# Gate and up products by Strassen's scheme (7 for 8), with the output projection of all tokens ahead of the FFN

## Chip, core and metric

The kernel runs on one NeuronCore of a Trainium2 chip. Its time is device microseconds, the median of several executions. A second view is one execution recorded by the hardware profiler; "the profile" and "the trace" below mean that one. PE is TensorE (PEld its weight loads), DVE VectorE, ACT ScalarE, POOL GpSimd, SP the engine whose queue issues the DMAs.

## What is computed

One inference step of a one-layer decoder: a mixer (four retention heads and four gated-delta heads on one normalised stream), an output projection, a layer norm, a SwiGLU feed-forward network (FFN), another layer norm. There are 2048 prompt tokens, 16 meta tokens (whose FFN output isn't asked for) and 32 sample tokens (8 x 4); D_MODEL is 1024, D_FF 2816. What matters here is the end:

```python
mixed = concatenate([o_r, o_g], -1) @ w_out            # 1024 x 1024
h = layer_norm(ALPHA * h + mixed, ln1_g, ln1_b)
gu = h @ w_gate_up                                     # 1024 x 5632
f = (silu(gu[..., :D_FF]) * gu[..., D_FF:]) @ w_down   # 2816 x 1024
y = layer_norm(ALPHA * h + f, ln2_g, ln2_b)
```

All inputs are float32. A matmul here takes each operand as a high part (a cast to float32r) and a low part (what is left), and adds three products, high x high, high x low, low x high. That is `mm3`; the split into two parts is `split`, a cast on ACT and a subtraction on DVE or POOL.

## The kernel before

`attention` goes first: four blocks of 512 prompt tokens, whose mixer outputs go to memory (`mixd`) with the normalised stream (`xhat`). Its code is the same before and after.

`ffn` then runs `ffn_block` for two blocks of tokens: 1056 (the 32 sample tokens and 1024 prompt tokens, nine tiles) and 1024 (eight tiles). A block has these stages:

- Output projection, a tile of 128 tokens at a time: `load(i)` brings the tile's mixer output and splits it, `project(i)` does 48 matmuls of 512 columns, adds the residual (L1105) and takes the layer norm, `transposed(i)` turns the tile on PE (L1113) and writes its split parts into `fxT`, which stays in SBUF for the block.
- Gate and up, for f from 0 to 21 (128 columns of gate and 128 of up each; the text calls one f a slice): `gateup(f)` loads 1 MB of weights as two raw halves, splits them (ACT, DVE), and for each group of 352 columns (first block) or 512 (second; 256 in the last two slices) does 2 x 24 matmuls into two PSUM tiles `g0` and `g1`; tanh on ACT (L1127) and two products on DVE (L1128, L1129) make the SwiGLU value, split on ACT and POOL into `ff`.
- Down, for each pair of slices: `down(g)` takes each tile and half of the model width, six matmuls of 512 columns, and adds to `y` on DVE (L1147). It runs behind the first slice of the next pair, so a whole slice of gate/up lies between its operands and its use.
- `finish(i)`: layer norm and store. In the second block the last two slices go in quarters with down and finish between them.

A layer norm (`layer_norm`) is two statistics (L212), a dozen one-column operations (L189 to L196, L225), an ACT pass (L228), a DVE product (L230) and two POOL additions (L232).

The order of instructions on each engine is not the order of the code: a scheduler lays them out at compile time, by the program's order as priority and by when it reckons that operands and buffers are ready. On the chip each engine takes its list strictly in that order. A tag with `bufs=n` has n buffers; a new tile of the tag waits until an old one has been read by all its readers. All DMAs are issued on SP.

Of the kernel before, what the change touches and what calls it, by code (L numbers as in the profile page):

```python
# [35 lines left out]
LAG = 3  # L36
# [112 lines left out]
class _Cut:  # L149


    def __init__(self, pool, full, n):
        self.pool, self.full, self.n = pool, full, n
# [10 lines left out]

class Builder:
# [124 lines left out]
    def mm3(self, out, lh, ll, rh, rl, kn, first=True, last=True):  # L290

        for k in range(kn):
            for i, (a, b) in enumerate(((lh, rh), (lh, rl), (ll, rh))):
                self.nc.tensor.matmul(out, lhsT=a(k), rhs=b(k), start=first and k == 0 and i == 0, stop=last and k == kn - 1 and i == 2)  # L294


    def setup(self):
        nc, I = self.nc, self.I
        cp = self.pool("const")
        self.wring = self.pool("wring", bufs=2)  # L300
        self.wcols = 8 * 264
        self.raw = self.pool("raw", bufs=2)
        self.dr = self.pool("dram", space=DRAM)
# [760 lines left out]
    def ffn_block(self, tiles, groups, bi):  # L1064

        nc = self.nc
        T = sum(r for _, r, _ in tiles)
        NT = len(tiles)
        TM = NS + 1024
        with ExitStack() as s:  # L1070
            xp, fp, tp = self.fxp, self.ffp, self.ftp
            pg, pd, pt = self.pg, self.pd, self.pt
            sm = self.fsm
            ff = lambda dt=F32: fp.tile([128, TM], dt, tag="ff", name="ff")
            y = [(self.fyp if i < 6 else xp).tile([128, D], F32, tag=f"y{i}", name=f"y{i}") for i in range(NT)]
            xT = xp.tile([128, 2, 8, TM], F32R, tag="fxT", name="fxT")
            xh, xl = xT[:, 0, :, :T], xT[:, 1, :, :T]
            vec = lambda i: self.vec_bcast(i, fp, "ff")
            mixed, wo = {}, {}

            def load(i):
                r0, rows, c0 = tiles[i]
                blk, off = self.mix_pos(r0)
                raw = ff()[:, :1024].rearrange("p (k n) -> p k n", k=8)[:, :, :rows]
                nc.sync.dma_start(out=raw, in_=self.mixd[blk][:, :, off:off + rows].rearrange("k p n -> p k n"))
                nc.sync.dma_start(out=y[i][:rows], in_=self.xhat_rows(r0, rows))
                if bi and i < NT // 2:

                    o = tiles[NT - 1 - i][2]
                    hh, ll = xh[:, :, o:o + rows], xl[:, :, o:o + rows]  # L1090
                else:
                    hh, ll = [ff(F32R)[:, :1024].rearrange("p (k n) -> p k n", k=8)[:, :, :rows] for _ in range(2)]
                self.split(raw, hh, ll, "act", "dve")
                mixed[i] = hh, ll

            def project(i):
                r0, rows, c0 = tiles[i]
# [8 lines left out]
                self.layer_norm(y[i][:rows], rows, g1, b1, sm)  # L1106

            def transposed(i):
                r0, rows, c0 = tiles[i]
                for j in range(2):  # L1110
# [3 lines left out]
                    self.split(p[:, :, :rows], xh[:, 4 * j:4 * j + 4, c0:c0 + rows], xl[:, 4 * j:4 * j + 4, c0:c0 + rows], "act", "dve")  # L1114

            def gateup(f, w=None, o=None, gs=None):
                wh, wl = w or self.piece(self.I["gu"][f])
                fh, fl = o or (ff(F32R)[:, :T], ff(F32R)[:, :T])
                for c, n in gs or groups:
                    ps = []  # L1120
                    for u in range(2):
                        p = pg.tile([128, 512], F32, tag=f"g{u}", name=f"g{u}")[:, :n]
                        ps.append(p)
                        q = 128 * u
                        self.mm3(p, lambda k: wh[:, k, q:q + 128], lambda k: wl[:, k, q:q + 128], lambda k: xh[:, k, c:c + n], lambda k: xl[:, k, c:c + n], 8)
                    t = tp.tile([128, 512], F32, tag="th", name="th")[:, :n]
                    nc.scalar.activation(out=t, in_=ps[0], func=AF.Tanh, scale=0.5)  # L1127
                    nc.vector.scalar_tensor_tensor(out=t, in0=t, scalar=1.0, in1=ps[0], op0=ALU.add, op1=ALU.mult)  # L1128
                    nc.vector.scalar_tensor_tensor(out=t, in0=t, scalar=0.5, in1=ps[1], op0=ALU.mult, op1=ALU.mult)  # L1129
                    self.split(t, fh[:, c:c + n], fl[:, c:c + n], "act", "pool")  # L1130
                return fh, fl

            def down(g, fs, w=None, sel=None, lag=0):
                wh, wl = w or self.piece(self.I["dn"][g])
                wv = [w.rearrange("p a b -> p (a b)") for w in (wh, wl)]
                for i in sel or range(NT):
                    r0, rows, c0 = tiles[i]
                    for n in range(2):
                        p = pd.tile([128, 512], F32, tag="d", name="d")[:rows]
                        o = 512 * n  # L1140
                        self.mm3(p, lambda f: fs[f][0][:, c0:c0 + rows], lambda f: fs[f][1][:, c0:c0 + rows],
# [6 lines left out]
                    if lag and i >= lag:  # L1148
                        finish(i - lag)

            def finish(i):
                r0, rows, c0 = tiles[i]
                self.layer_norm(y[i][:rows], rows, g2, b2, sm, bi and i == NT - 1)
                nc.sync.dma_start(out=self.O["y"][r0:r0 + rows, :], in_=y[i][:rows])

            for n in range(2):
                for kk in range(2):
                    wh, wl = self.piece(self.I["wout"][n, kk])
                    r = lambda w: w.rearrange("p a b -> p (a b)").rearrange("p (a b) -> p a b", a=4)
                    wo[n, kk] = r(wh), r(wl)  # L1160
                    if n + kk == 0:
                        load(0)
            load(1)
            g1, b1 = vec(2), vec(3)
            for i in range(NT):
                project(i)
                if i and i + 1 < NT:
                    load(i + 1)
                if i > bi:
                    transposed(i - bi - 1)  # L1170
                if self.late:
                    self.late.pop(0)()

            ng = NF // 2
            w = self.piece(self.I["gu"][0])
            f0 = ff(F32R)[:, :T], ff(F32R)[:, :T]
            gateup(0, w, f0, groups[:-1])
            for i in range(NT - bi - 1, NT):
                transposed(i)
            gateup(0, w, f0, groups[-1:])  # L1180
            fs = [f0, gateup(1)]
            for g in range(ng - 1):
                if g == ng - 2:
                    g2, b2 = vec(4), vec(5)
                    if bi:
                        break
                nxt = [gateup(2 * g + 2)]
                down(g, fs)
                nxt.append(gateup(2 * g + 3))
                fs = nxt  # L1190
            if bi:

                w = [self.piece(self.I["gu"][NF - 2 + u]) for u in range(2)]
                down(ng - 2, fs)
                fs = [(ff(F32R)[:, :T], ff(F32R)[:, :T]) for u in range(2)]
                wd = self.piece(self.I["dn"][ng - 1])
                q = T // 4
                for i in range(4):
                    for u in range(2):
                        gateup(NF - 2 + u, w[u], fs[u], [(q * i, q)])  # L1200
                        if i:
                            down(ng - 1, fs, wd, [2 * i - 2 + u])
                            if 2 * i - 2 + u:
                                finish(2 * i - 3 + u)
                for i in (6, 7):
                    down(ng - 1, fs, wd, [i])
                    finish(i - 1)
                finish(NT - 1)
            else:
                down(ng - 1, fs, lag=LAG)  # L1210
                self.late = [lambda i=i: finish(i) for i in range(NT - LAG, NT)]

# [13 lines left out]
    def piece(self, src):  # L1226
        self.np = getattr(self, "np", 0) + 1
        return self.load_piece(src, ring=self.wring if self.np % 2 else self.wring2)

    def ffn(self):  # L1230
        with ExitStack() as s:
            self.wring2 = self.pool("wring2", bufs=2, es=s)
            self.ffp = self.pool("f_f", bufs=7, es=s)
# [34 lines left out]
```

## Time and profile before

| what | value |
|---|---|
| time, median of 3 runs | 3127.39 us (3121.61 to 3128.01) |
| the profiled execution's own time | 3126.54 us |
| its span, first to last instruction | 3124.8 us |
| mean granted TensorE clock | 0.982 |
| PE, PEld busy | 2992.5 us (96%), 2589.8 us (83%) |
| DVE, ACT, POOL busy | 1708.0 (55%), 882.4 (28%), 548.6 us (18%) |
| first output-projection matmul | at 1348.2 us |
| moved by DMA | 309.41 MB, 99 GB/s in the mean |

A busy PE in this table is not PE at its peak, since matmuls overlap in the record; the distance from one matmul's start to the next one's is the better measure. A digit of the page's slices is the busy tenth of one fortieth of the span, 78 us. An idle time "<- DVE y L1147" was ended by that instruction.

### The profile page before, as it was taken

The page shows a single profiled execution, that of the slowest core. Times are in us where ns is not written, and L with a number is a line of the kernel's source. Part 1 is how long each engine was busy: PE and PEld are TensorE (multiplying, and loading weights), DVE is VectorE, ACT ScalarE, POOL GpSimd, SP SyncE. Part 2 cuts the span into 40 slices and gives each one's busy share as a digit, 9 for nine tenths or more (in the row PEclk, how much of TensorE's full clock was granted, in tenths as well). Part 3 has the DMA queues.
Part 4 walks back from the last instruction along what each step waited for, and adds up shares of the span by engine and source line. Part 5 has one row for each costly group of instructions (what it writes and reads, how often), then busy time and mean ns, then how long its engine had stood idle before and what let it go on. Part 6 is the DMA issues. An engine that isn't in the chain of part 4 may idle for free. (4 is left out here: it accounts for less than half of the span.)

```text
span 3124.8 us, 44640 instructions
## 1 busy us (share of the span) xinstructions
PE 2992.5 (96%) x17858; PEld 2589.8 (83%) x17858; DVE 1708.0 (55%) x3922; ACT 882.4 (28%) x2083; POOL 548.6 (18%) x570
## 2 busy tenths in 40 slices
PE   7999998999999989999999999999999999999997
PEld 6888887888888877878999999988777877878787
DVE  7777676766666676667333333333684333333346
ACT  2444433444443434333111111111233111111111
POOL 1332222221222131112101111110241000001002
PEclk8999998999999999999999999999999999999999
DMA  7534543443434333252111111112242111111111
GB/s 255 222 139 173 179 151 127 149 147 144 154 144 149 117 116 117 92 167 75 41 54 41 41 52 44 41 46 63 84 134 81 41 54 41 54 41 54 41 41 55
DMA packets 96592, 309.41 MB, mean 99 GB/s; under 512 B 11472, under 2 KB 39680, under 8 KB 80000
## 3 DMA queue, kind: packets, MB, share of 16 engines
q1 hardware_dynamic: 96384, 306.56, 27.8%
q8 instruction: 140, 2.29, 0.3%
q14 instruction: 68, 0.56, 0.1%
HBM read 242.40 MB, written 64.13 MB: 98 GB/s over the span
## 5 line engine op out<-in xcount | busy, mean ns | idle before, releaser
L294 PE MATMUL g<-fxT,wh 128*128 128x352 f32 (+2 forms) x3648 | 955.1, 344 | 1.4 <-DVE th L1128 0.6
L294 PEld LDWEIGHTS g<-fxT,wh 128*128 128x128 f32 x3648 | 646.7, 188 | 62.8 <-ACT fxT L237 1.0
L294 PE MATMUL d<-wh,ff 128*128 128x512 f32 (+1 forms) x1912 | 617.2, 397 | 15.7 <-DVE y L1147 6.8
L294 PE MATMUL g<-fxT,wl 128*128 128x352 f32 (+2 forms) x1824 | 627.0, 344 | 0.0
L294 PE MATMUL pj<-wh,xT 128*128 128x256 f32 (+2 forms) x2176 | 457.9, 298 | 9.1 <-ACT wh L237 3.6
L294 PEld LDWEIGHTS d<-wh,ff 128*128 128x128 f32 (+1 forms) x1912 | 350.5, 183 | 116.2 <-DVE y L1147 16.7
L294 PE MATMUL d<-wl,ff 128*128 128x512 f32 (+1 forms) x956 | 377.8, 395 | 1.7 <-DVE wl L244 1.7
L294 PE MATMUL pj<-xT,wh 128*128 128x512 f32 (+1 forms) x1280 | 377.1, 378 | 0.8 <-DVE kp L702 0.6
L244 POOL TENSOR_TENSOR ff<-th,ff 128x352 fp32r<-128x352 f32 (+2 forms) x114 | 142.8, 1252 | 1299.1 <-ACT ff L237 1223.4
L294 PEld LDWEIGHTS pj<-wh,xT 128*128 128x128 f32 (+1 forms) x2176 | 357.0, 192 | 14.6 <-ACT wh L237 3.9
L294 PEld LDWEIGHTS g<-fxT,wl 128*128 128x128 f32 x1824 | 342.5, 188 | 28.8
L237 ACT CAST wh<-raw 128x1024 fp32r<-128x1024 f32 x180 | 184.5, 1049 | 627.7 <-PE d L294 407.6
L1147 DVE TENSOR_TENSOR y<-y,d 128x512 f32<-128x512 f32 (+1 forms) x340 | 231.7, 685 | 187.3 <-PE d L294 187.2
L294 PE MATMUL pj<-wl,xT 128*128 128x256 f32 (+3 forms) x1088 | 317.4, 292 | 0.5 <-POOL wl L244 0.5
L244 DVE TENSOR_TENSOR wl<-raw,wh 128x1024 fp32r<-128x1024 f32 x178 | 235.6, 1340 | 45.8 <-ACT wh L237 44.3
L1128 DVE SCALAR_TENSOR_TENSOR th<-th,g 128x352 f32<-128x352 f32 (+2 forms) x114 | 65.2, 572 | 339.0 <-ACT th L1127 339.0
L1129 DVE SCALAR_TENSOR_TENSOR th<-th,g 128x352 f32<-128x352 f32 (+2 forms) x114 | 65.2, 572 | 336.3 <-PE g L294 336.2
L294 PE MATMUL pj<-xT,wl 128*128 128x512 f32 (+1 forms) x640 | 228.3, 357 | 0.0
L294 PEld LDWEIGHTS pj<-xT,wh 128*128 128x128 f32 x1280 | 206.7, 191 | 19.6 <-DVE S L601 3.0
L294 PEld LDWEIGHTS d<-wl,ff 128*128 128x128 f32 (+1 forms) x956 | 175.4, 184 | 44.9 <-DVE wl L244 2.6
L294 PEld LDWEIGHTS pj<-wl,xT 128*128 128x128 f32 (+1 forms) x1088 | 209.4, 192 | 1.3 <-POOL wl L244 0.8
L1127 ACT ACTIVATE th<-g 128x352 f32<-128x352 f32 (+2 forms) x114 | 57.7, 506 | 372.1 <-PE g L294 343.4
(272 smaller groups left out, 3778.6 us busy)
## 6 DMA issues: line engine op xcount, KB each, us to landing
wh<-parts SPq DMA_DIRECT2D x45, 1024.0 KB, 6.1
wl<-parts SPq DMA_DIRECT2D x45, 1024.0 KB, 6.7
raw<-gu SPq DMA_DIRECT2D x88, 512.0 KB, 3.9
raw<-dn SPq DMA_DIRECT2D x44, 512.0 KB, 4.1
parts<-wh SPq DMA_DIRECT2D x15, 1024.0 KB, 6.2
parts<-wl SPq DMA_DIRECT2D x15, 1024.0 KB, 7.2
raw<-wret SPq DMA_DIRECT2D x16, 512.0 KB, 6.8
raw<-wgd SPq DMA_DIRECT2D x16, 512.0 KB, 6.4
```

Source lines behind the costliest of these rows:

```text
L237: i = nc.scalar.copy(out=h, in_=src)
L244: i = (nc.vector if el == "dve" else nc.gpsimd).tensor_tensor(out=l, in0=src, in1=h.bitcast(F32), op=ALU.subtract)
L294: self.nc.tensor.matmul(out, lhsT=a(k), rhs=b(k), start=first and k == 0 and i == 0, stop=last and k == kn - 1 and i == 2)
L1127: nc.scalar.activation(out=t, in_=ps[0], func=AF.Tanh, scale=0.5)
L1128: nc.vector.scalar_tensor_tensor(out=t, in0=t, scalar=1.0, in1=ps[0], op0=ALU.add, op1=ALU.mult)
L1129: nc.vector.scalar_tensor_tensor(out=t, in0=t, scalar=0.5, in1=ps[1], op0=ALU.mult, op1=ALU.mult)
L1147: nc.vector.tensor_tensor(out=ys, in0=ys, in1=p, op=ALU.add)
```

## The change

The output projection becomes a stage of its own, `project`, over all 17 tiles with one load of its weights. A tile's normed tokens go to memory (`yd`). Transposed tiles are taken in pairs A and B. Of the halves of their 1024 features (lo, hi), four differences are made on POOL, and seven operands are split and stored in memory (`bd`): b11 = A lo, b21 = A hi, b22 = B hi, t1 = B lo - A lo, t2 = B hi - t1, t3 = B hi - B lo, t4 = A hi - t2.

The FFN then has three blocks of tokens: 544 (four prompt tiles and the sample tokens, 272 columns for each of A and B) and twice 768 (384 columns). A block loads its seven operands. For each slice, `weights(f)` makes four sums of the weight quarters on POOL (s1 to s4 out of a11 = gate lo, a21, a12, a22) and splits the seven weight operands; `gateup` does seven products of 12 matmuls, adding up in four PSUM tags X, Y, Z, W and with five additions on DVE, and gets gate and up for A and B. `between` is the down projection of the pair before, as a generator: three of its steps (six matmuls, one addition) behind each product of the next slice. The last block's down has no slice to go beside.

`mm3` takes `more` for products that add to a bank already in use. The DMA scratch is cut to 1024 so that the tiles fit.

```diff
+BLOCKS = [
+    Block([(_P(0), _P(1), 128), (_P(2), _P(3), 128), (0, NS // 2, NS // 2)]),
+    Block([(_P(i), _P(i + 1), 128) for i in (4, 6, 8)]),
+    Block([(_P(i), _P(i + 1), 128) for i in (10, 12, 14)]),
+]
+ORDER = ("b11", "t2", "b21", "t1", "t3", "t4", "b22")
...
-    def ffn_block(self, tiles, groups, bi):
+    def project(self):
...
-                self.split(raw, hh, ll, "act", "dve")
+                self.split(raw, hh, ll, "act", "pool")
...
+            def sums(bi, j, ra, rb, w):
...
+                sub = lambda o, x, z: nc.gpsimd.tensor_tensor(out=o, in0=x, in1=z, op=ALU.subtract)
+                sub(T[:, 0], B[:, lo], A[:, lo])
+                sub(T[:, 2], B[:, hi], B[:, lo])
+                sub(T[:, 1], B[:, hi], T[:, 0])
+                sub(T[:, 3], A[:, hi], T[:, 1])
...
+                for src, names in parts:
+                    m = 4 * len(names)
+                    h, l = [cp.tile([128, 8, 128], F32R, tag=t, name=t)[:, :m, :w] for t in ("ch", "cl")]
+                    self.split(src, h, l, "act", "dve")
+                    for u, name in enumerate(names):
+                        for v, part in enumerate((h, l)):
+                            nc.sync.dma_start(out=BLOCKS[bi].stored(self.bd[bi, name], v, j, w), in_=part[:, 4 * u:4 * u + 4, :].bitcast(F32))
...
+            def weights(f):
...
+                r0, r1 = halves(I["gu"][f])
+                a11, a21, a12, a22 = r0[:, :, :128], r0[:, :, 128:], r1[:, :, :128], r1[:, :, 128:]
+                S = sp.tile([128, 4, 4, 128], F32, tag="S", name="S")
+                op = lambda o, x, z, f: nc.gpsimd.tensor_tensor(out=o, in0=x, in1=z, op=f)
+                op(S[:, 0], a21, a22, ALU.add)
+                op(S[:, 1], S[:, 0], a11, ALU.subtract)
+                op(S[:, 2], a11, a21, ALU.subtract)
+                op(S[:, 3], a12, S[:, 1], ALU.subtract)
+                w = {}
+                w["a11"] = parts(a11, "a11", 2)
+                s12 = parts(S[:, 0:2].rearrange("p a k n -> p (a k) n"), "s12")
+                w["a12"] = parts(a12, "a12")
+                s34 = parts(S[:, 2:4].rearrange("p a k n -> p (a k) n"), "s34")
+                w["a22"] = parts(a22, "a22")
...
+                def product(p, a, b, more=False):
+                    (ah, al), v = w[a], B[b]
+                    self.mm3(p, lambda k: ah[:, k], lambda k: al[:, k], lambda k: blk.moving(v, 0, k), lambda k: blk.moving(v, 1, k), 4, not more, True, more)
+                    for _ in range(3):
+                        next(between, None)
...
+                product(X, "a11", "b11")
+                nc.scalar.copy(out=x1, in_=X)
+                product(Y, "s2", "t2")
+                add(u2, x1, Y)
+                product(X, "a12", "b21", more=True)
+                product(Z, "s1", "t1")
+                product(Y, "s3", "t3", more=True)
+                add(u3, x1, Y)
+                add(c22, u3, Z)
+                product(W, "a22", "t4")
+                add(u3, u3, W)
+                swish(X, u3, 0, "ta")
+                product(Z, "s4", "b22", more=True)
+                add(u2, u2, Z)
+                swish(u2, c22, 1, "tb")
...
+            w = weights(0)
+            between = iter(())
+            for bi, blk in enumerate(BLOCKS):
+                B = {}
+                for name in ORDER:
+                    t = bp.tile([128, 2 * 4 * 384], F32R, tag=name, name=name)[:, :8 * blk.n]
+                    nc.sync.dma_start(out=t.bitcast(F32), in_=self.bd[bi, name])
+                    B[name] = blk.shaped(t)
...
+                for f in range(NF):
+                    nxt = weights((f + 1) % NF) if f + 1 < NF or bi + 1 < len(BLOCKS) else None
+                    fs.append(gateup(blk, B, w, between))
+                    w = nxt
+                    between = iter(())
...
+                    if f % 2:
+                        g = f // 2
+                        end = g == ng - 1
+                        between = down(blk, g, fs, downw(g), y, end and ("end" if bi + 1 == len(BLOCKS) else "block"))
```

Buffers of the FFN stage: one for each operand of a block, two of a11, one of s12, a12, s34, a22 and S, four raw halves for all weights, one pair of down weights, three of each of fh and fl, one of each y tile; PSUM two of X, one of Y, Z, W, three for down. In `swish` the SwiGLU value is made as before, and split on ACT and POOL. After its last pair of slices `down` takes the layer norm and stores each tile as its steps end.

More of the change, by code (lines that the diff above doesn't have):

```diff
@@ L1061, in turned @@
             yield
-    def ffn_block(self, tiles, groups, bi):
[L1066 to L1069, printed above, removed]
-        with ExitStack() as s:
[L1071 to L1079, printed above, removed]
+    def project(self):
+        nc, I = self.nc, self.I
+        with ExitStack() as s:
+            w2 = self.pool("wring2", bufs=2, es=s)
+            op = self.pool("o_m", bufs=2, es=s)
+            yp = self.pool("o_y", bufs=4, es=s)
+            xp = self.pool("o_x", bufs=3, es=s)
+            tp = self.pool("o_t", bufs=1, es=s)
+            cp = self.pool("o_c", bufs=2, es=s)
+            vp = self.pool("o_v", es=s)
+            sm = self.pool("o_sm", bufs=2, es=s)
+            pd = self.pool("p_d", bufs=3, space=PSUM, es=s)
+            pt = self.pool("p_t", bufs=3, space=PSUM, es=s)
+            wo = {}
+            work = [(bi, t) for bi, blk in enumerate(BLOCKS) for t in blk.tiles()]
+            mixed, y, xr = {}, {}, {}
@@ L1086, in load @@
                 nc.sync.dma_start(out=y[i][:rows], in_=self.xhat_rows(r0, rows))
[L1087 to L1092, printed above, removed]
-                self.split(raw, hh, ll, "act", "dve")
+                hh, ll = [op.tile([128, 8, 128], F32R, tag=t, name=t)[:, :, :rows] for t in ("mh", "ml")]
@@ L1106, in project @@
                 self.layer_norm(y[i][:rows], rows, g1, b1, sm)
+                nc.sync.dma_start(out=self.yd[bi][BLOCKS[bi].row(r0):BLOCKS[bi].row(r0) + rows, :], in_=y[i][:rows])
             def transposed(i):
-                r0, rows, c0 = tiles[i]
+                bi, (r0, rows) = work[i]
+                x = xr[r0] = xp.tile([128, 8, 128], F32, tag="xr", name="xr")
                 for j in range(2):
@@ L1133, in down @@
[L1133 to L1137, printed above, removed]
+                    nc.scalar.copy(out=x[:, 4 * j:4 * j + 4, :rows], in_=p[:, :, :rows])
+                del y[i]
+                blk = BLOCKS[bi]
+                for j, (ra, rb, w) in enumerate(blk.pairs):
+                    if r0 == rb or (ra == rb - w and r0 == ra and w == NS // 2):
+                        sums(bi, j, ra, rb, w)
@@ new lines, in project @@
+            for n in range(2):
+                for kk in range(2):
+                    self.np = getattr(self, "np", 0) + 1
+                    wh, wl = self.load_piece(I["wout"][n, kk], ring=self.wring if self.np % 2 else w2)
+                    r = lambda w: w.rearrange("p a b -> p (a b)").rearrange("p (a b) -> p a b", a=4)
+                    wo[n, kk] = r(wh), r(wl)
+                    if n + kk == 0:
+                        load(0)
+            load(1)
+            g1, b1 = self.vec_bcast(2, vp, "g1"), self.vec_bcast(3, vp, "b1")
@@ L1147, in down @@
                             nc.vector.tensor_tensor(out=ys, in0=ys, in1=p, op=ALU.add)
[L1148 to L1211, printed above, removed]
@@ L1213, in mix_pos @@
+            for _ in between:
+                pass
     def mix_pos(self, r0):
```

191 lines of the change are left out of this document (145 added, 46 removed).

## The prediction

> **What bounds the kernel now.** I read the head of the page and its slices first, then the groups of instructions by form from 1300 us on, the chain that ended last, windows by stage, and timelines of a few microseconds.
>
> ```profile
> span 3124.8 us, 44640 instructions
> PE   7999998999999989999999999999999999999997
> DVE  7777676766666676667333333333684333333346
> ...
> 400.00:800.00 400.00, 377.99 (x2702) 326.85 (x2703) 268.48 (x793) 161.86 (x488) 85.66 (x105) 0.97 0.38 139
> 2200.00:2300.00 100.00, 93.98 (x442) 77.61 (x441) 81.68 (x203) 28.57 (x33) 30.82 (x24) 0.98 0.45 144
> 2260.00:2280.00 20.00, 17.61 (x70) 13.89 (x69) 19.51 (x51) 7.73 (x7) 6.50 (x6) 0.91 0.89 289
> 2300.00:2400.00 100.00, 94.25 (x427) 76.36 (x426) 64.32 (x145) 32.30 (x40) 28.52 (x20) 0.98 0.24 79
> 2500.00:3000.00 500.00, 495.68 (x2130) 398.27 (x2129) 184.41 (x229) 77.36 (x101) 41.47 (x29) 1.00 0.14 48
> 3100.00:3125.00 25.00, 6.47 (x27) 4.61 (x25) 17.92 (x52) 2.48 (x2) 7.50 (x7) 0.70 0.20 84
> ```
>
> The window columns are stretch, PE, PEld, DVE, ACT, POOL busy, granted clock, DMA share, GB/s. The FFN (slices from about 1400 us) is TensorE's alone: PE 495.68 of 500 us at clock 1.00, DVE 184.41. PE idles at three places only: 11.8 us between the two token blocks (2200 to 2400, where DVE is full), 18.5 us after 3100, and in the attention part (22 us of 400), where DVE is busy 67%.
>
> Pipelined matmuls overlap in the record, so I take their spacing, not their duration: first and last of 72 matmuls of 352 columns, then pieces of the chain.
>
> ```profile
> L294 PE MATMUL g<-fxT,wh 128*128 128x352 f32 x2112 | 506.3, 322 | 1.4 <-DVE th L1128 0.6 <-ACT fxT L237 0.6 <-DVE fxT L244 0.2
> L294 PE MATMUL g<-fxT,wh 128*128 128x512 f32 x1280 | 402.7, 395 | 0.0
> L294 PE MATMUL g<-fxT,wh 128*128 128x256 f32 x256 | 46.0, 281 | 0.0
> ...
> 1561.14 0.48 PE L294 MATMUL g<-fxT,wh 128*128 128x352 f32 x2
> 1572.67 0.48 PE L294 MATMUL g<-fxT,wh 128*128 128x352 f32 x2
> ...
> 2319.60 11.15 PE d L294 x48
> 2330.75 0.87 PE tr L1113 x8
> 2588.10 43.64 PE g L294 x188
> 3058.27 5.69 PE g L294 x48
> 3063.96 2.78 PE d L294 x12
> ```
>
> Spacing: 352 columns (1572.67-1561.14)/72 = 160.1 ns; 512 columns 43.64/188 = 232.1 ns; 256 columns 5.69/48 = 118.5 ns; a down matmul 2.78/12 = 231.7 ns.
>
> **Term 1, the products.** Before: each row of wh matmuls has half as many wl ones beside it, so 3168 x 160.1 + 1920 x 232.1 + 384 x 118.5 ns = 998.3 us. After: 7 products x 12 matmuls = 84 a slice (one of the 22 values of f), at 272 columns in the first block and 384 in the two others. Straight between the neighbours: 272 at 125.4 ns, 384 at 174.5 ns; 1848 x 125.4 + 3696 x 174.5 = 876.7 us. **-121.6 us.** If 272 costs no more than 256, 13 us less; if reading columns in three runs of 128 costs something, the nearest row (the contiguous 352) gives no price, and I allow 13 us the other way. The 17 x 2 down steps for each of 11 pairs, the 17 x 48 projection matmuls (11.15 us a tile) and the transposes (0.87) are the same matmuls before and after: zero, as PE bounds both.
>
> The other terms need the helpers' durations.
>
> ```profile
> L1147 DVE TENSOR_TENSOR y<-y,d 128x512 f32<-128x512 f32 x320 | 218.9, 686 | 187.2 <-PE d L294 187.0
> L237 ACT CAST wh<-raw 128x1024 fp32r<-128x1024 f32 x148 | 151.2, 1049 | 608.5 <-PE d L294 407.6 <-PE g L294 172.5 <-DMA raw<-gu 16.9
> L212 DVE BATCH_NORM_STATS2 lnst<-y 128x6 f32<-128x512 f32 x64 | 43.8, 684 | 0.8
> L230 DVE TENSOR_TENSOR y<-y,ff 128x1024 f32<-128x1024 f32 x31 | 39.7, 1284 | 8.4 <-ACT y L228 8.2
> L228 ACT ACTIVATE y<-y,lnnm,rqy 128x1024 f32<-128x1024 f32 x31 | 38.3, 1243 | 89.6 <-DVE lnnm L225 64.4 <-issue 24.9
> L1129 DVE SCALAR_TENSOR_TENSOR th<-th,g 128x352 f32<-128x352 f32 x66 | 34.4, 521 | 167.2 <-PE g L294 167.0
> L195 DVE SCALAR_TENSOR_TENSOR rqt<-rqy,rqa 128x1 f32<-128x1 f32 x96 | 26.3, 280 | 2.0
> L1127 ACT ACTIVATE th<-g 128x352 f32<-128x352 f32 x66 | 30.7, 465 | 175.6 <-PE g L294 146.9 <-POOL ff L244 28.6
> ...
> L244 POOL TENSOR_TENSOR wl<-raw,wh 128x1024 fp32r<-128x1024 f32 x2 | 4.7, 2363 | 10.2 <-ACT wh L237 10.2
> ...
> raw<-gu SPq DMA_DIRECT2D x88, 512.0 KB, 3.9
> ```
>
> And a stretch of the timeline in which DVE and POOL meet, with the end of the kernel:
>
> ```profile
> 2497.50 1.23 DVE L244 TENSOR_TENSOR wl<-raw,wh 128x1024 fp32r<-128x1024 f32 x1 [0.17 <-ACT wh L237]
> 2499.01 1.29 POOL L244 TENSOR_TENSOR ff<-th,ff 128x512 fp32r<-128x512 f32 x1 [10.74 <-ACT ff L237]
> 2499.22 0.40 PE L294 MATMUL g<-fxT,wh 128*128 128x512 f32 x1
> 2499.24 2.15 DVE L244 TENSOR_TENSOR wl<-raw,wh 128x1024 fp32r<-128x1024 f32 x1
> 2499.46 0.42 PE L294 MATMUL d<-wh,ff 128*128 128x512 f32 x1
> ...
> 3112.59 2.48 POOL L232 TENSOR_TENSOR y<-y,ff 128x512 f32<-128x512 f32 x2 [10.49 <-DVE rqy L196]
> 3112.62 1.25 DVE L225 SCALAR_TENSOR_TENSOR lnnm<-lnmv,rqy 128x1 f32<-128x1 f32 x1
> ```
>
> The same DVE subtraction took 1.23 us alone and 2.15 us begun under a POOL operation, and a one-column operation took 1.25 us: a DVE operation that reads only SBUF waits for POOL's to end. The Trainium skill (SBUF — State Buffer, Who interferes with whom) says that a DVE instruction with two SBUF inputs and a GpSimd one that reads SBUF exclude each other, the later fully blocked; the trace agrees in these two places. It speaks against this change, which gives POOL four sums a slice; the sum below charges half a POOL operation for each meeting, and rival B the whole.
>
> **Term 2, slices in steady state.** A pair of slices (two gate/up, one down) costs PE 2 x 84 x 0.1254 + 10 x 1.39 = 35.0 us in block 0, 46.0 in the others. For each slice the helpers gain: weights split in three blocks instead of two and 7 x 512 columns instead of 2048 (DVE 3.5 x 1.23 = 4.3 us), four POOL sums (4 x 1.29), five DVE additions out of PSUM (0.43 us at 272 columns, 0.56 at 384, scaled from 521 ns at 352), which nothing in the old kernel did. ACT's copy of the first product (0.5) has product 2 as cover even behind a cast of 1.05 (1.7 with the handover against 1.5 and 2.1): zero. Two places have less.
> (a) Product 7 adds to the bank that the fifth product's two additions must have read. They take 0.2 + 2 x 0.43 + 0.2 = 1.3 us against 1.5 us of product 6 (1.5 against 2.1 in the wide blocks). In front of them on DVE can stand the next slice's s12 split, released by product 4: ACT 1.05, DVE 1.23, done 2.3 us after product 4 where the addition could start after 1.7. About 0.4 us a slice in block 0, none in the wide ones.
> (b) Odd slices have no down steps beside them, and the next step of PE after product 1 is down, which wants the new tiles and both halves of the down weights. In block 0 that is 8 x 1.5 = 12.0 us; DVE owes 4.3 + 2.5 (down weights) + 9 x 0.43 = 10.7, and about ten of its operations meet POOL (busy 6.7 of the 12.0 us) for 0.6 us each: 3.4. Late by 2.1 us a pair. In the wide blocks DVE fits into 16.8 us, but the second half's chain (add 0.56, tanh 0.5, two products 1.1, cast 0.5, POOL 0.97, handovers of 0.17) is 4.7 us against product 1 and two down steps, 4.9: with the s34 split (1.23) or a POOL sum (1.29) ahead, 1.1 us late a pair.
> Sum: 11 x (2.1 + 0.8) + 22 x 1.1 = **+56 us**. Bounds: 10 (PE's order bends round each wait, as the g matmul at 2499.22 among d matmuls does) to 110.
>
> **Term 3, projection of all 17 tiles.** PE 12.0 us a tile. POOL: split 2.36, norm 2 x 1.29, half of four differences 2.6 = 7.5 us; DVE's SBUF-only work 1.23 + half of 3.5 x 1.23 + 1.5 small = 4.9. Together 12.4, as they exclude each other: about 0.9 us over a tile, **+15 us** (0 to 35). The moved DMAs (14 part stores a pair, a token store a tile) go out on SP behind splits; nobody reads them soon. Saved: half of the wout splits, hidden before.
>
> **Term 4, projection to FFN.** By the tile sizes, laid out pool after pool (my assumption), the raw weights of slice 0 lie where the last pair's transposed tokens are. After the last projection matmul: addition 0.7, norm 8.7 (statistics 1.4, a dozen one-column operations 2.2, ACT 1.24, DVE 1.28, POOL 2.6), transposes 0.9, copy 0.6, four POOL differences 5.2, splits 3.5, load 3.9, split 1.2: the first product starts some 25 us on, the second waits 3.7 more for two sums and a split. PE has two tiles' transposes and one product in it: **+26 us** (15; to 45 if the seven operands, 7.8 MB, come one at a time at the 134 GB/s of the raw<-gu row).
>
> **Term 5, block borders.** Each operand has one buffer: 11 MB must come between product 1 of the last slice and product 7 of the next, some 39 us; with 4 MB of weights that is 52 us at the best rate seen, 289 GB/s. DVE owes about 68 us (five or six norms of 4.9) for 54 of PE over those slices. On SP, in order, weight loads queue behind an operand load that waits for its buffer. They overlap: 16 us a border, 32 in all, less the 11.8 of the one border before: **+20** (-5 to +45).
>
> **Term 6, the end.** Nothing lies beside the last down. Six tiles of DVE work, 2 x 0.686 + 2 x 0.684 + 1.28 + 2.2 = 6.2 us each, 3 us of start, 4 of store and end, 7 of meetings with POOL: 51 us, in which PE has 16.7. Idle 34 against 18.5: **+16** (5 to 28).
>
> **The sum.** 3126.5 (the profiled run; span 3124.8, and 0.9 under the median 3127.4) - 121.6 + 56 + 15 + 26 + 20 + 16 = 3137.9, on the median's footing 3139: I say **3140**, 0.4% slower. This kernel's runs differ by 0.2%, about what a measurement can tell from no change.
>
> **Rivals.** A, faster: PE's order hides the steady waits. The other terms leave -45 us, so it decides where the steady stall falls under 39 us, 1.2 us a pair; at the lower bound, 10 us, the time is 3093, and 3055 with the other terms at half. For: PE's 495.68 of 500, the bent order. Against: DVE was at 37% there, and comes to some 70 to 80%.
> B, much slower: DVE and POOL, excluding each other, set the pace as in the attention part, where PE is idle 22 of 400 us at DVE 67%: 5.5% of 1400 us is 77, and with whole meetings 110; with terms 3, 5 and 6 at 35, 35, 28 the time is 3240. For: the DVE row 2.15. Against: both together need 27 of block 0's 35 us, 29 of 46 in the others.
> C: the operands come late and PE's clock falls in the gaps (0.91 at 2260 to 2280): terms 4 and 5 at their upper ends, 3184.
>
> **Numbers.** Forecast with its own range 3121 to 3170: 0.38. A 0.37, B 0.13, C 0.12. Faster 0.37, all A; same 0.09, the lower edge of the forecast; slower 0.54. Between 3065 and 3225 lie all but 2 in 10: A's tail with several low ends at once, and B's.
>
> **What would show it.** The g products spaced 125 and 174 ns in 1848 and 3696 matmuls (else term 1 fails); PE idle before product 7 put to DVE additions, and before d matmuls in odd-to-even turns, 1 to 3 us a pair (else A); SBUF-only DVE operations well over 1.23 us (B, if over 1.8 in the mean); a hole of 25 us at one place near 1570 us (term 4); two holes of some 16 us with DVE full (5); 50 us after the last g matmul (6). I am wrong if PE is busy 99% over the slices, or if the borders alone cost over 50 us.

## The result and the profile after

The changed kernel takes 3316.70 us (median; 3309.36 to 3318.67). The kernel before, run on the same chip beside it, takes 3124.50 (3119.47 to 3128.01). The ratio is 1.0612 with a 95% interval of 1.0588 to 1.0637: 6.1% slower. The forecast was 3140 with a range of 3065 to 3225: slower was right, with a chance of 0.54 on record for it, but the size is far off.

The profiled execution took 3309.36 us, 183 more than that of before. From its page, the head and the engines; from the windows, a stretch of the narrow first block and one of a wide block (columns as in the prediction):

```profile
span 3307.6 us, 47037 instructions
PE 2966.0 (90%) x17930; PEld 2620.6 (79%) x17930; DVE 2260.4 (68%) x4529; ACT 1112.2 (34%) x2499; POOL 1089.7 (33%) x927
...
1650.00:2050.00 400.00, 341.54 (x2004) 302.21 (x2003) 264.95 (x347) 115.22 (x209) 153.94 (x121) 0.91 0.21 68
2150.00:2550.00 400.00, 367.94 (x1800) 333.68 (x1799) 261.48 (x323) 107.94 (x169) 146.32 (x97) 0.95 0.22 74
```

Where PE was busy 495.68 of 500 us at clock 1.00 before, it is now busy 92% at 0.95 in the wide blocks and 85% at 0.91 in the narrow one. DVE is at 65 to 66%, POOL at 37 to 38%: neither is full.

PE's waits after 1350 us (line, waited for, us in total, times, longest):

```profile
PE d L363 <- POOL fl L313: 76.5, 33, 3.9
PE Z L363 <- DVE c L1302: 49.1, 32, 4.1
PE X L363 <- DMA fr<-gu: 24.9, 1, 24.9
PE d L363 <- ACT fh L306: 19.7, 21, 1.3
PE tr L1183 <- POOL oy L301: 13.7, 2, 9.1
PE d L363 <- DVE oy L1173: 8.5, 4, 3.8
```

The first two are the prediction's places (b) and (a): down waits once a pair for the low part of the last SwiGLU value (`fl`), product 7 waits for the additions that must have read bank Z. The price of one is 2.3 us in the mean in (b) and up to 4.1 in (a). The groups of instructions behind them:

```profile
L1268 POOL TENSOR_TENSOR S<-fr 128x512 f32<-128x512 f32 x132 | 206.5, 1583 | 77.9 <-DVE s34l L313 55.3 <-DMA fr<-gu 22.5
L1268 POOL TENSOR_TENSOR S<-S,fr 128x512 f32<-128x512 f32 x66 | 112.0, 1697 | 0.5
L313 DVE TENSOR_TENSOR a11l<-fr,a11h 128x512 fp32r<-128x512 f32 x66 | 103.7, 1572 | 11.2 <-ACT a11h L306 11.2
L1310 DVE SCALAR_TENSOR_TENSOR tb<-tb,c 128x384 f32<-128x384 f32 x44 | 67.3, 1529 | 0.2
L313 POOL TENSOR_TENSOR fl<-tb,fh 128x384 fp32r<-128x384 f32 x44 | 64.6, 1468 | 6.8 <-ACT fh L306 6.8
```

The POOL sums of these two groups take 1.6 and 1.7 us in the mean, and the two DVE operations that meet them two to three times what they take without POOL's sums (0.69 and 0.57 us, shown below). How one such wait comes about, in the timeline of a wide turn from an odd slice to an even one:

```profile
3110.05 3.23 POOL L1268 TENSOR_TENSOR S<-fr 128x512 f32<-128x512 f32 x2 [1.37 <-DVE s34l L313]
3110.36 1.78 DVE L313 TENSOR_TENSOR a11l<-fr,a11h 128x512 fp32r<-128x512 f32 x1
3112.06 1.64 DVE L1310 SCALAR_TENSOR_TENSOR tb<-tb,c 128x384 f32<-128x384 f32 x1
3113.25 1.59 POOL L1268 TENSOR_TENSOR S<-S,fr 128x512 f32<-128x512 f32 x1
3113.73 0.51 ACT L306 CAST fh<-tb 128x384 fp32r<-128x384 f32 x1 [3.05 <-DVE tb L1310]
3114.30 0.50 PE L363 MATMUL d<-dh,fh 128*128 128x512 f32 x1 [1.04 <-ACT fh L306]
3114.92 1.26 POOL L1268 TENSOR_TENSOR S<-fr,S 128x512 f32<-128x512 f32 x1
3116.14 0.99 POOL L313 TENSOR_TENSOR fl<-tb,fh 128x384 fp32r<-128x384 f32 x1
3117.18 0.79 PE L363 MATMUL d<-dh,fl 128*128 128x512 f32 x1 [2.15 <-POOL fl L313]
3117.77 0.84 PE L363 MATMUL Y<-t,s12h 128*128 128x384 f32 x2
3118.73 0.84 PE L363 MATMUL Y<-t,s12h 128*128 128x384 f32 x2
...
3112.00:3117.00 5.00, 1.99 (x8) 1.02 (x6) 2.90 (x4) 0.51 (x1) 4.92 (x4) 0.94 0.21 60
3117.00:3122.00 5.00, 4.82 (x14) 4.67 (x15) 0.77 (x2) 0.00 (x0) 0.13 (x1) 0.50 0.11 45
```

All four sums of the next slice stand in POOL's list ahead of `fl`. The first two hold DVE's split of a11 and then the product that makes `tb`; the cast comes at 3113.73; `fl` is ready to go at 3114.24 and starts at 3116.14, behind the last two sums. PE waits 1.04 and 2.15 us, with 0.7 us of matmuls between the two waits. Then comes what the prediction didn't count: the granted clock is 0.50 for the next five microseconds (last row), and three matmuls of 384 columns take 3118.73 - 3117.77 = 0.96 us, 320 ns each, where they take 174 at full clock. (A row with x2 merges two matmuls; a third one, of the low part, lies between the two rows.) The down matmuls are back at full speed only at 3122.9.

The whole difference can be laid out against PE's own pace (matmuls at the spacings of the prediction: 204 us of projection with its transposes, 876.7 or 998.3 of products, 520 of down). From the first projection matmul to the end of the span, before: 3124.8 - 1348.2 = 1776.6 us, 54 over its pace of 1722. After: 3307.6 - 1344.4 = 1963.2, 362 over its pace of 1601. The parts of the 362 lie between these matmuls:

| stretch of after | us | PE's pace | over it |
|---|---|---|---|
| projection, 1344.4 to 1559.7 | 215.3 | 202 | 13 |
| to the first product, 1604.2 | 44.6 | 2 | 43 |
| narrow block, to 2098.7 | 494.5 | 371 | 123 |
| two wide blocks, to 3263 | 1164.3 | 1009 | 155 |
| the last down and the end, to 3307.6 | 44.6 | 17 | 28 |

(A block's first slices have less down beside them; the paces allow for it.) In the wide blocks a steady pair of slices takes 51.6 us instead of 46.0: 22 x 5.6 = 123, and what is left of the 155, about 32, is put down to the borders. So -121.6 of products, +308.2 of losses (362.2 less 54.0), and 3.8 less ahead of the projection give the 183.

### The profile page after: what moved, and what is told of

Read it like the earlier page. It is cut to its first block, busy times and chain, and to the rows that moved or that the text cites. A ratio compares the mean times of both kernels' runs of the same rounds, so it can differ in the third digit from the quotient of the medians.

```text
span 3307.6 us, 47037 instructions
## 1 busy us (share of the span) xinstructions
PE 2966.0 (90%) x17930; PEld 2620.6 (79%) x17930; DVE 2260.4 (68%) x4529; ACT 1112.2 (34%) x2499; POOL 1089.7 (33%) x927
## 4 chain that ended last, share of the span: by engine, by line
PE 58%; DVE 22%; POOL 8%; ACT 5%; issue 4%; DMA 3%; SPq 0%; POOLq 0%; ACTq 0%; DVEq 0%
PE pj L363 16%; PE d L363 13%; PE Y L363 6%; POOL S L1268 6%; PE X L363 5%; PE Z L363 5%; PE W L363 2%; DVE s12l L313 1%; DVE rqt L264 1%; POOL fl L313 1%; DVE lnst L281 1%; DMA bd<-ch 1%; DVE s34l L313 1%; DVE u L1302 1%; DVE cacc L817 1%
## 5 line engine op out<-in xcount | busy, mean ns | idle before, releaser
L363 PE MATMUL d<-dh,fl 128*128 128x512 f32 (+1 forms) x748 | 305.2, 408 | 76.5 <-POOL fl L313 76.5
L363 PE MATMUL d<-dh,fh 128*128 128x512 f32 (+1 forms) x748 | 301.5, 404 | 21.0 <-ACT fh L306 19.7
L363 PE MATMUL d<-dl,fh 128*128 128x512 f32 (+1 forms) x748 | 298.1, 399 | 0.0
L363 PEld LDWEIGHTS d<-dh,fl 128*128 128x128 f32 (+1 forms) x748 | 141.2, 189 | 124.9 <-POOL fl L313 90.9
L1268 POOL TENSOR_TENSOR S<-fr 128x512 f32<-128x512 f32 x132 | 206.5, 1583 | 77.9 <-DVE s34l L313 55.3
L363 PEld LDWEIGHTS d<-dh,fh 128*128 128x128 f32 (+1 forms) x748 | 142.6, 191 | 59.4 <-ACT fh L306 29.8
L363 PE MATMUL Z<-b,s34h 128*128 128x384 f32 (+1 forms) x528 | 138.4, 348 | 49.2 <-DVE c L1302 49.1
L363 PEld LDWEIGHTS d<-dl,fh 128*128 128x128 f32 (+1 forms) x748 | 141.6, 189 | 28.7
L363 PE MATMUL Y<-t,s12h 128*128 128x384 f32 (+1 forms) x528 | 153.4, 381 | 2.7 <-DVE u L1302 1.5
L917 POOL TENSOR_TENSOR Lm<-LT,lvl 128x512 f16<-128x512 f32 (+1 forms) x108 | 138.4, 1314 | 34.9 <-DVE LT L905 28.4
```

What stands on the lines that cost most here:

```text
L917: nc.gpsimd.tensor_tensor(out=Lm[:, x - 1], in0=LT, in1=lvl(x), op=ALU.mult)
L1268: op = lambda o, x, z, f: nc.gpsimd.tensor_tensor(out=o, in0=x, in1=z, op=f)
```

## The experiments

The kernel before ran beside them at 3124.31 to 3125.55 us (median).

### What the POOL sums cost: four kernels

**Sums left out.**

```diff
-                op(S[:, 0], a21, a22, ALU.add)
-                op(S[:, 1], S[:, 0], a11, ALU.subtract)
-                op(S[:, 2], a11, a21, ALU.subtract)
-                op(S[:, 3], a12, S[:, 1], ALU.subtract)
+                q0, q1 = [r.rearrange("p a (u n) -> p (a u) n", u=2) for r in (r0, r1)]
...
-                s12 = parts(S[:, 0:2].rearrange("p a k n -> p (a k) n"), "s12")
+                s12 = parts(q0, "s12")
...
-                s34 = parts(S[:, 2:4].rearrange("p a k n -> p (a k) n"), "s34")
+                s34 = parts(q1, "s34")
```

> The four weight sums on POOL are left out; s1 to s4 are split straight from the raw quarters, so every cast, subtraction, addition and matmul stays, on other values. Theory 1 (POOL): POOL's remaining 2 splits a slice meet DVE rarely, the waits in front of down and of product 7 shrink below 1 us and the clock stays up: 150 to 220 us gained, 3100 to 3165 us. Theory 2 (DVE's work): DVE has the same work, less than 50 us gained. Theory 3 (the chain behind the last product is simply longer than the one product of cover): the narrow block gains its 4 us wait and its clock, some 70 us, the wide ones keep theirs, about 3240.

3094.16 us; to before 0.9905 (0.989 to 0.992). That is 222 us less than after, a little more than theory 1 forecast. **Sums on DVE**, the same sums, added to the busier engine:

```diff
-                op = lambda o, x, z, f: nc.gpsimd.tensor_tensor(out=o, in0=x, in1=z, op=f)
+                op = lambda o, x, z, f: nc.vector.tensor_tensor(out=o, in0=x, in1=z, op=f)
```

> The four weight sums go from POOL to DVE, 2.5 us more DVE work a slice, none of it shut out by POOL any more except by the two fl splits. Theory 1 (POOL and its hold on DVE): faster than the changed kernel, by 50 to 120 us, because a sum costs DVE 0.6 us and a meeting with POOL cost it about as much. Theory 2 (DVE's work): slower than the changed kernel, 2.5 us a slice where DVE is full, 60 us or more in the narrow block alone.

3125.44 us; 1.0000 (0.9990 to 1.0009). 191 us less than after, more than expected, with more work on DVE than after. From the pages, groups and windows of the kernel without sums (first three lines) and that with sums on DVE (the rest):

```profile
L313 DVE TENSOR_TENSOR a11l<-fr,a11h 128x512 fp32r<-128x512 f32 x66 | 45.3, 687 | 46.4 <-ACT a11h L306 46.4
L1305 DVE SCALAR_TENSOR_TENSOR tb<-tb,c 128x384 f32<-128x384 f32 x44 | 25.1, 572 | 0.2
2100.00:2550.00 450.00, 449.02 (x2345) 416.95 (x2344) 282.71 (x452) 138.17 (x214) 42.60 (x42) 1.00 0.26 92
...
PE 2887.8 (93%) x17930; PEld 2553.4 (82%) x17930; DVE 2282.2 (73%) x4793; ACT 1111.6 (36%) x2499; POOL 682.4 (22%) x663
L1268 DVE TENSOR_TENSOR S<-fr 128x512 f32<-128x512 f32 x132 | 90.3, 685 | 7.4 <-DMA fr<-gu 7.4
2100.00:2550.00 450.00, 445.31 (x2313) 410.38 (x2312) 341.23 (x499) 136.54 (x214) 56.69 (x40) 1.00 0.26 89
PE Y L363 <- DVE u L1302: 30.4, 34, 4.0
PE d L363 <- POOL fl L313: 8.5, 15, 1.2
```

DVE is busy 22 us longer in all than after and PE far less held: DVE's load is not the cause. What counts is that no sum runs on POOL, ahead of `fl` or beside a DVE operation. The same sum takes 0.69 us on DVE against 1.58 on POOL, and the split of a11 falls from 1.57 to 0.69 us.

Without sums PE runs at the spacing that the prediction took. Matmul starts in the kernel without sums:

```profile
1774.21 0.42 PE L363 MATMUL X<-b,a11h 128*128 128x272 f32 x2
1775.35 0.41 PE L363 MATMUL X<-b,a11h 128*128 128x272 f32 x2
...
2435.55 0.51 PE L363 MATMUL X<-b,a11h 128*128 128x384 f32 x2
2437.11 0.51 PE L363 MATMUL X<-b,a11h 128*128 128x384 f32 x2
2481.67 0.51 PE L363 MATMUL X<-b,a11h 128*128 128x384 f32 x2
```

Nine matmuls lie between the rows of each of the first two pairs: 1.14/9 = 127 ns at 272 columns, 1.56/9 = 173 at 384. A pair of slices takes 2481.67 - 2435.55 = 46.1 us; the sum of the prediction's terms for PE was 46.0.

**Only `fl` on DVE**, the sums stay on POOL. It tells POOL's order (`fl` behind the sums) from the exclusion of DVE and POOL.

```diff
-  self.split(t[:, c:c + m], fh[:, o:o + m], fl[:, o:o + m], "act", "pool")
+  self.split(t[:, c:c + m], fh[:, o:o + m], fl[:, o:o + m], "act", "dve")
```

> The subtraction that makes fl goes from POOL to DVE, the weight sums stay on POOL. It parts theory 1 in two. If the wait in front of down comes from POOL's queue (fl stands behind the sums), it goes, 5 us a pair in the wide blocks, and the narrow block's wait in front of product 7 stays: 3180 to 3230. If it comes from POOL's hold on DVE (each DVE operation out of SBUF waits up to 1.7 us for a sum to end), the chain stays as late, and DVE has two such operations more: 3270 or over.

3190.62 us; 1.0224 (1.0196 to 1.0252): 126 of the 191. PE's waits:

```profile
PE Y L363 <- DVE u L1302: 43.2, 29, 2.8
PE d L363 <- ACT fh L306: 21.1, 27, 1.1
```

So both halves are there. The queue behind four sums is the larger; the rest comes on DVE's chains, which still meet the sums (a wide pair 48.8 us against 46.8 with the sums on DVE). That this rest is the exclusion alone is likely, not shown apart from DVE's extra work.

**Down later.** Products 1 and 2 have no down steps behind them, so the late chains have two products of cover more.

```diff
-                def product(p, a, b, more=False):
+                def product(p, a, b, more=False, steps=3):
...
-                    for _ in range(3):
+                    for _ in range(steps):
...
-                product(X, "a11", "b11")
+                product(X, "a11", "b11", steps=0)
...
-                product(Y, "s2", "t2")
+                product(Y, "s2", "t2", steps=0)
```

> The down steps start behind product 3 of the next slice instead of product 1; all work stays. In the changed kernel a pair of slices takes 51.6 us in the wide blocks (46.0 at PE's pace) and 46.3 in the narrow one (35.0), 247 us over all 33 pairs. Theory 1 (POOL: the split fl of the second half stands behind the weight sums on POOL and behind POOL's hold on DVE, PE waits about 3 us for it in front of down, and its clock then falls to 0.50 for some 6 us): the wide blocks lose their wait and with it the slow clock, 5 us a pair, 110 us; the narrow block keeps the wait in front of product 7; in all about 3190 to 3220 us. Theory 2 (DVE has too much work, whatever waits for it): the wait moves to another place, less than 40 us gained, 3280 or more.

3154.27 us; 1.0091 (1.0074 to 1.0109). 162 us less than after with every POOL sum in its place, 36 better than the range that was expected; a wide pair takes 45.9 us, PE's pace. So DVE and POOL, with all their meetings, don't set the pace of the wide blocks: the chain to `fl` was too long for its cover. The wait for `fl` falls from 76.5 to 14.6 us in all. The narrow block still takes about 41 us a pair, with waits at (a):

```profile
PE Z L363 <- DVE c L1302: 21.8, 10, 2.3
PE d L363 <- POOL fl L313: 14.6, 12, 3.8
```

### The clock after a wait

**More work in the wait.** In 32 slices product 1 is done once more into bank W before the down steps; nothing reads that result. It adds 384 matmuls, (10 x 12 x 125.4 + 22 x 12 x 174.5 ns) = 61 us at full clock.

```diff
+                    if fill and a == "a11":
+                        self.mm3(W, lambda k: ah[:, k], lambda k: al[:, k], lambda k: blk.moving(v, 0, k), lambda k: blk.moving(v, 1, k), 4)
                     for _ in range(3):
                         next(between, None)
...
+                fill = hasattr(between, "gi_frame")
```

> The changed kernel with more work: in the 32 slices that have a down beside them, product 1 is done a second time, into bank W, whose content nobody reads (product 6 overwrites it), between product 1 and the down steps. That is 61 us of matmuls more, put where PE waits some 3 us for fl. If PE's clock falls to 0.50 because of that wait (theory 1), the wait shrinks to about 1 us, the clock stays up, and the kernel gets faster though it does more: 2 us a pair in the wide blocks, 2 to 3 in the narrow one, 40 to 75 us, 3240 to 3275. If the low clock has another reason, the filler only takes the place of waiting, and the time stays within 15 us of 3316; if the wait only moves behind the filler, it is slower, up to 3375.

3265.68 us; 1.0447 (1.0429 to 1.0466): 51 us faster than after with 61 us more to do, so 112 us of loss are gone. Engines and a wide stretch of this kernel, and its waits for `fl`:

```profile
PE 2983.2 (91%) x18314; PEld 2651.7 (81%) x18314; DVE 2246.0 (69%) x4529; ACT 1112.8 (34%) x2499; POOL 1096.1 (34%) x927
2100.00:2550.00 450.00, 427.36 (x2192) 392.15 (x2191) 308.14 (x432) 129.22 (x198) 180.39 (x115) 0.98 0.24 79
PE d L363 <- POOL fl L313: 35.7, 25, 3.7
```

The waits for `fl` fall by 41 us. The granted clock rises from 0.95 to 0.98 in these wide stretches, and from 0.94 to 0.97 between the first product and the last; over the 1659 us that these take in after, that is some 50 us more. Most of the rest is shorter waits elsewhere (those for `fh` fall from 19.7 to 2.0 us). So the low clock comes from the waits: the sums and DVE's work are the same here, PE has more to do, and it is granted more.

### The hole between projection and FFN

**Other addresses.** The FFN's pools are laid out in another order, so that the weight buffers no longer lie where the projection's last tiles are.

```diff
             bp = self.pool("f_b", es=s)
+            yp = self.pool("f_y", es=s)
+            hp = self.pool("f_h", bufs=3, es=s)
+            wp = self.pool("f_w", es=s)
+            tp = self.pool("f_t", es=s)
+            sm = self.pool("f_sm", bufs=2, es=s)
+            vp = self.pool("f_v", es=s)
             ap = self.pool("f_a", es=s)
             rp = self.pool("f_r", bufs=4, es=s)
             sp = self.pool("f_s", es=s)
-            wp = self.pool("f_w", es=s)
-            hp = self.pool("f_h", bufs=3, es=s)
-            yp = self.pool("f_y", es=s)
-            tp = self.pool("f_t", es=s)
-            sm = self.pool("f_sm", bufs=2, es=s)
-            vp = self.pool("f_v", es=s)
```

> Only the order in which the FFN's buffers are laid out changes: the weight buffers lie beyond what the projection stage uses, so that slice 0's weights can come before that stage ends. All work stays. If the hole between projection and FFN (44 us from the last projection matmul to the first product) is set by the raw weights that wait for the last pair's transposed tokens, it falls to 10 to 20 us and the kernel gains 25 to 35 us. If it is set by the seven operands (7.8 MB), it stays above 35 us and the gain is under 10.

3309.36 us; 1.0599 (1.0582 to 1.0617): 7 us won of the 25 to 35 expected. After, the raw weights were issued on SP only behind the last pair's stores (first row); with the pools moved the first product starts at 1587.31, 17 us earlier, and the wait for `b21` in front of product 3 takes much of it back (the other rows, PE's and SP's timelines of this kernel):

```profile
1597.91 1.27 SPq L1254 DMA_DIRECT2D fr<-gu  x2
...
1587.31 0.82 PE L363 MATMUL X<-b,a11h 128*128 128x272 f32 x2 [0.68 <-ACT xr L1184]
1613.35 0.79 PE L363 MATMUL X<-b,a12h 128*128 128x272 f32 x2 [19.86 <-DMA b<-bd]
1605.44 0.64 SPq L1357 DMA_DIRECT2D b<-bd  x1
```

The hole has two causes, the weights' buffers and the operands that return from memory; with the first gone, the second holds almost as long. In both kernels the load that PE waits for was issued on SP behind the last pair's stores, which block 0 doesn't need: 12 of the 19.86 us had passed when `b21` was issued at 1605.44, and the product began 7.9 us later.

**Operand loads on ACT's queue**, in the first block, on top of the best version below.

```diff
-                    nc.sync.dma_start(out=t.bitcast(F32), in_=self.bd[bi, name])
+                    (nc.sync if bi else nc.scalar).dma_start(out=t.bitcast(F32), in_=self.bd[bi, name])
```

> The version with sums on DVE, late down and moved weight buffers (3067), and the first block's seven operand loads issued from ACT's queue instead of SP's. In that version the first product starts 22 us after the last projection matmul and product 3 waits 18 us more for b21, whose load was issued on SP behind the last tile's stores, 25 us after the two before it. If SP's order holds the loads back, the two holes shrink together from 40 to some 20 us: 3045 to 3055. If the memory or the transfer itself is what takes long (7.8 MB), 3060 to 3070.

3078.65 us; 0.9853 (0.9831 to 0.9875): 11 us slower than the same kernel with the loads on SP, outside both ranges that were expected. Now another operand comes late, the one of product 6 (`t4`). The seven loads go out one by one between 1564.67 and 1609.28, in ACT's list, among casts that wait up to 11.46 us for a buffer whose store has not landed:

```profile
PE W L363 <- DMA t<-bd: 11.9, 1, 11.9
...
1595.27 0.62 ACT L306 CAST ch<-xr 128x512 fp32r<-128x512 f32 x1 [11.46 <-DMA bd<-ch]
1609.28 0.33 ACTq L1357 DMA_DIRECT2D b<-bd  x1
```

So this edit puts one list in order in place of another, and doesn't tell the order of the loads from their transfer. How much of the wait is the transfer's stays open; the window of after between projection and first product moves 297 GB/s at a DMA share of 0.85.

### Strassen or the stages?

**Plain products.** Eight ordinary products of four operands in the new stages, without differences, sums or additions.

```diff
-ORDER = ("b11", "t2", "b21", "t1", "t3", "t4", "b22")
+ORDER = ("b11", "b21", "b12", "b22")
...
+                product(X, "a11", "b11")
+                product(X, "a12", "b21", more=True)
+                product(Y, "a21", "b11")
+                product(Y, "a22", "b21", more=True)
+                swish(X, Y, 0, "ta")
+                product(Z, "a11", "b12")
+                product(Z, "a12", "b22", more=True)
+                product(W, "a21", "b12")
+                product(W, "a22", "b22", more=True)
+                swish(Z, W, 1, "tb")
```

> The new stages stay (projection first, operands in memory, three blocks), but the FFN goes back to eight products: gate and up, A and B, each of 24 matmuls; no differences, no weight sums, no additions on DVE, four operands instead of seven. A pair of slices at PE's pace is 50.2 us in the wide blocks and 38.0 in the narrow one. If the loss of the changed kernel is in Strassen's helpers (theory 1), PE runs here at its pace: 22 x 50.2 + 11 x 38.0 us for the slices, 122 us above the kernel without sums (3094), less some 20 us for fewer operands at the hole and the borders: 3180 to 3215, 100 to 135 us faster than the changed kernel though it has 125 us more matmuls. If the loss is in the new stages, it takes more than the changed kernel, 3320 and over. Against the kernel before, its excess is what the new stages cost by themselves: 55 to 90 us.

3133.97 us; 1.0042 (1.0027 to 1.0056). The expectation missed by 46: with four operands the hole is 27 us instead of 45, the borders cost almost nothing, and the pairs run at the pace of 96 matmuls a slice (49.9 us wide). Its wide stretch:

```profile
2100.00:2550.00 450.00, 450.00 (x2383) 423.00 (x2382) 191.06 (x307) 99.39 (x163) 39.08 (x38) 1.00 0.24 78
```

So the stages and three blocks alone cost about 10 us, and the loss of after is all the scheme's: its differences, its sums, its additions and its seven operands.

**Sums stored.** Sums on DVE in the first block alone, kept in memory and read back in the two others; the blocks in the order wide, wide, narrow; pools moved.

```diff
+                if bi:
+                    nc.sync.dma_start(out=flat, in_=self.sd[f])
+                else:
...
+                    nc.sync.dma_start(out=self.sd[f], in_=flat)
```

> The weight sums are made once, on DVE in the first block, written to memory (1 MB a slice) and read back in the two others; a wide block goes first and the narrow one last; weight buffers laid beyond the projection's. The second and third block then have the helpers of the kernel without sums, which ran its pairs in 46.1 and 35.7 us. From 3125 (sums on DVE in every block): 0.7 us a pair in one wide block, 1.4 in the narrow one, a shorter end (five tiles instead of six) and a shorter hole: 3070 to 3100 us, faster than the kernel before. If the loads (2.5 MB a slice) come late, the pairs lengthen by 2 us or more and it is 3130 or over.

3128.88 us; 1.0015 (1.0002 to 1.0029): a miss. The wide pairs run at some 45.7 us once the sums come from memory, but the pairs of the narrow block, now last, take 38 to 43, and the hole stays (`t<-bd`, 21.8 us). Against the kernel with sums on DVE the two wide blocks win 10 us (1050 for 1061), and the narrow one, which now has a border in front of it, loses 38 (446 for 408). Why its pairs stay above the 37 us of the kernel without sums stays open.

### A version that beats both

**Sums on DVE, down later, pools moved** (three of the edits above).

> Three edits at once: weight sums on DVE, down behind product 3, weight buffers laid beyond the projection's. If the late start of down helps where DVE makes the sums as it did with POOL's, by hiding what is left of the waits in front of down and of product 5 (some 45 us of idle time in the kernel with sums on DVE), 3085 to 3110 us. If DVE's load is what is left, it does not help: 3115 to 3130.

**3067.32 us**; 0.9826 (0.9803 to 0.9850), 57 us below before. A wide stretch, and the longest waits that are left of those in the FFN:

```profile
2650.00:3000.00 350.00, 350.00 (x1837) 326.53 (x1837) 256.31 (x381) 106.55 (x165) 41.09 (x31) 1.00 0.20 65
PE X L363 <- DMA b<-bd: 18.3, 1, 18.3
PE Y L363 <- DVE u L1302: 10.8, 13, 2.2
```

PE is busy 350.00 of 350 us with DVE at 256.31. The gain is a little under half of term 1. From the first projection matmul on this kernel is 114 us over PE's pace, against 54 before: 38 at the hole (20 to the first product, 18.3 for `b21`), 28 at the end, 19 in the rest of the narrow block, 18 in the wide ones, 10 in the projection. Its expectation was beaten by 18 us.

## Why the prediction was wrong, point by point

**Term 1, right.** 84 matmuls a slice at 127 and 173 ns, against 125.4 and 174.5: the -122 us is there. Columns read in three runs cost nothing that shows.

**Term 2 failed, in size: 246 us where 56 stood**, 123 for 32 in the narrow block and 123 for 24 in the wide ones, above even its upper bound of 110. The places were right, and so were the waits' releasers. Three things were mis-sized or left out:

- *Half a POOL operation a meeting.* A POOL sum takes 1.58 or 1.70 us in the two groups shown, not the 1.29 of the row it was taken from, and the two DVE operations on the way to `fl` take 0.9 to 1.0 us more in the mean (a11l 1.57 for 0.69, the product tb 1.53 for 0.57), where half of 1.29 was charged. Rival B's "mean over 1.8 us" was too high a mark: these two more than doubled, while the large s34l stayed at 1.23. B was nearer in the price of a meeting, but not in its mechanism: the two engines don't set the pace of the wide blocks, since with down later and every meeting kept these run at 45.9 us a pair.
- *POOL's own order.* The prediction counted 0.97 us for `fl` with one sum ahead in the worst case. The four sums of the next slice stand ahead. With `fl` taken off POOL, 126 us go.
- *The clock.* It was in the forecast only for gaps at the borders (rival C). In the steady slices such a wait was followed by a stretch at half clock, 6.8 us in the turn shown; by the trace's clock records, 18 of the 25 such stretches in the wide blocks last 3.4 us and the others 6.8. By the excess of the low-clock matmuls over their normal spacing this is some 2 us more a pair in the wide blocks and 3 in the narrow one, an estimate of 75 to 85 of the 246. (The granted clock is 0.94 over the 1659 us from the first product to the last, which bounds the loss at 100.) The kernel with a filler shows that it follows from the wait.

Place (a) was put at none in the wide blocks and 0.4 us a slice in the narrow one. It is 49 us in all, 38 of them in the narrow block: the four operations ahead of the addition on DVE are not one s12 split of 1.23 us but splits stretched to 1.4 to 2.0 us each.

**Term 3, about right**: 13 us over PE's pace in the projection, against 15; of these 8.5 are waits for the addition (`oy` L1173) in its second half, at 1474.5 to 1552.7.

**Term 4**: 43 where 26 was taken, just within the upper bound of 45. The address clash was rightly read, but it isn't the last wait: take it away and the operands hold the products 20 us. What term 4 lacks is SP's list, in which the loads of block 0 stand behind the last pair's stores.

**Term 5, right in kind**: about 32 us at both borders, less 11.8, is +20, as forecast; the 32 is a remainder, but at the first border (2085 to 2165) PE idles 13 of 80 us with DVE busy 70. **Term 6**: 44.6 us after the last product against 51, idle 28 for 34.

Rival A fell: PE's order did bend (the high-part matmuls of down go ahead while `fl` is missing), and it doesn't reach further than a step or two. But where down stands two products later, the steady stall of the wide blocks is gone: whether A holds was a matter of cover.

## What to carry to other kernels

A chain that ends in a matmul should have as much cover as the longest queue ahead of each of its links, in whole operations, and bulk work that nobody waits for soon does not belong on the engine that holds one of the links: here moving the sums from POOL to the busier DVE won 191 us. In this kernel a TensorE wait of about 3 us cost one and a half to two times its length (a wide pair is 5.6 us over PE's pace, with waits of 3.2 in the turn shown), for the clock falls behind it; two short ones close together counted as one. Before a scheme saves an eighth of the matmuls, count its extra operands too: what remains of the gain in the best version is half, and most of the other half goes at the edges of the stages.

## What the runs showed of the hardware

The granted clock in this trace is 1.00 or 0.50, and values between are means over longer windows. At 0.50, 384 columns take 320 ns a matmul against 174, for 5.7 us (3117.2 to 3122.9) behind two waits of 1.04 and 2.15 us with 0.7 us of matmuls between them. The Trainium skill (TensorE: Matmul & The Clock Gate, What's actually happening) says that the clock passes either half or all of its pulses and falls after an idle window of some 3.4 us; the half agrees with the 0.50 of the window (the spacing grows by 1.8, not by 2), and here two waits, each shorter than that window, were enough together.

A kernel with 61 us more matmuls ran 51 us faster, since they stood in the place of waits and kept the clock up. And a sum of 512 columns that takes 0.69 us on DVE takes 1.58 on POOL beside DVE's work: here even an engine that is two thirds full was the better place for it.
